# Fixed places for activations and weights, and a longer ordered TensorE table, in a hybrid decoder layer

## The chip, the cores and the metric

The kernel runs on one core of one Trainium2 chip, as one program in one launch. The metric is the device time of one execution in microseconds (us); smaller is better. Engines are called PE (TensorE matmul), PEld (its weight load), DVE (VectorE), ACT (ScalarE), POOL (GpSimd) and SP (the queue that issues most transfers). "L177" is line 177 of the kernel before.

## What is computed

One decoder layer on 256 tokens of width 2048, in float32 (the reference, cut):

```
h = rms_norm(x, attn_norm_g);  proj = h @ w_in                       # 2048 x 4448
r, k, v, w, a, g = split(token_shift(proj[:, :3360], mu))            # RWKV-7 group, 16 heads x 64
y_rwkv = rwkv7_mixer(...)        # a recurrent state per head, group norm, bonus term, gate
c_q, c_kv, k_pe = split(proj[:, 3360:])                              # latent attention, 8 heads x 128
q = rms_norm(c_q) @ w_uq;  kv = rms_norm(c_kv) @ w_ukv               # 512 -> 1536 and 512 -> 2048
y_mla = softmax(causal(q_nope k_nope^T + rope(q_pe) rope(k_pe)^T)) v
x = x + concat(y_rwkv, y_mla) @ w_out                                # 2048 x 2048
h = rms_norm(x, ffn_norm_g)
gate = causal_depthwise_conv3(h @ w_gate);  up = h @ w_up            # 2 x (2048 x 5632)
x = x + (silu(gate) * up) @ w_down                                   # 5632 x 2048
out = rms_norm(x, final_norm_g)
```

## The kernel before

Weights come from HBM in pieces of 128 x 1024 float32 (512 KB). `piece()` loads one into `raw` (SP queue, 3 buffers), ACT casts it to `hi` (L138, the fp32r rounding) and DVE subtracts to get `lo = raw - hi` (L139); `hi` and `lo` have 3 buffers each. Activations are split into the same two halves. A product is then three PE products (hi by hi, hi by lo, lo by hi), each matmul with a 128 x 128 stationary operand that PEld loads and a moving operand of 256 or 512 columns:

- Input projection (`in_tile`, `latent_tile`, L196/L199/L822): the weights are stationary, the activations `x` move, 256 columns at a time.
- Up projections of the latent attention (`up_b`, L896): the weights are stationary, the latents `cl` move, 256 columns.
- Value projection and output projection (`part_a`, L837): the activations (`cl`, `yhi`, `ylo`) are stationary, the weights move, 512 columns.
- First FFN product, gate and up (`prod_b`, L177 for `hi`, 512 columns of `z` hi and lo together; L183 for `lo`, 256 columns). `runs_of` fixes how many `hi` matmuls come ahead of each group of eight `lo` matmuls.
- Down product (`prod_a`, L219 to L221): the activations `hh`, `hl` are stationary, the weights move, 512 columns.

The FFN goes in two blocks, of 24 and 20 tiles of 128 hidden columns; each block is a gate/up stage and then a down stage. PSUM accumulators of the big products are `mm` (3 buffers), small steps use `ch` (3) and `at` (2).

Buffers with the tag `a8` hold 8 x 256 float32 per partition and rotate over four places; in turn they hold the four tiles of `x`, then `qn`, `kn`, `yhi`, `ylo` (second half of the attention output), then the four tiles of `z` (the normed input of the FFN, before its scale), then four weight pieces `wt` that are split early. A counter moves every second one by 32 elements (128 bytes). All other tiles of 1024 elements are `s4`.

Between the input projection and the FFN, PE runs an order that is written out by hand. `STREAM` lists the big products (`l` latent tiles, `q K Q` up projections, `v` values, `W` output projection, first digit the half of the mixed width, second the block of 512 output columns); each is a generator that yields every 8 matmuls of 256 columns or every 4 of 512. `PLAN` says how many such yields to take and which small step comes then: `R` and `T` (`corner_r`, `corner_t`: 32 x 32 matmuls that finish the inverse of the recurrence; `R` reads `T11`, which comes from DRAM through `dU`, L636 to L638), `w x i s u o` (the recurrence by chunks of 64 tokens), `r b` (norms of the latents), `c e` (rotary part), `S P A` (scores, transposes of the probabilities, attention times values), `N G Y` (group norm, gate, transposes of y), `X` (`turn_x`: transposes of the new x into `z`) and `g` (four loads on the ACT queue). The FFN follows that table, where the tile scheduler places it.

The second norm's factor `rs2B` is needed to scale the results of the gate/up product when they leave PSUM (`joined`), not to start it; it is computed after the table on POOL (`rsqrt` without an engine) and spread by two small matmuls (`bcast`, L262).

Of the kernel before, what the change touches and what calls it, by code (L numbers as in the profile page):

```python
# [54 lines left out]
def hybrid_layer(ctx: ExitStack, tc: tile.TileContext, a: dict, out: bass.AP):  # L55
# [73 lines left out]

    def piece(src, dst=None):  # L130
# [7 lines left out]
        S.copy(hi, raw)  # L138
# [24 lines left out]


    def prod_b(n, src, act, done):


        pcs, accs, g = {}, {}, 0
        for q, run in enumerate(runs_of(2 * n)):
            for _ in range(run):  # L170
                p, j = divmod(g, 8)
                i, h = divmod(p, 2)
                if j == 0:
                    pcs[p] = piece(src(i, h))
                    if h == 0:
                        accs[i] = mm()
                PE.matmul(accs[i], pcs[p][0][:, j * P:(j + 1) * P], act(h * 8 + j), start=h == 0 and j == 0,  # L177
                          stop=False, skip_group_check=True)
                g += 1
            i, h = divmod(q, 2)  # L180
            lo = pcs.pop(q)[1]
            for j in range(8):
                PE.matmul(accs[i][:, :T], lo[:, j * P:(j + 1) * P], act(h * 8 + j)[:, 0, :], start=False,  # L183
                          stop=h == 1 and j == 7, skip_group_check=True)
            if h == 1:
                done(i, accs.pop(i))

    def runs_of(n):
        full, tail = (10, 8) + (9, 9, 6) * 7 + (6,), (10, 8, 9, 6, 9, 9, 6, 7)
        return full * (n // 24) + tail * (n % 24 // 8)  # L190

# [698 lines left out]
    def up_b(src, i, x, dsts):  # L890
        pcs = piece(a[src][i])
        accs = [mm() for _ in range(2)]
        ops = [(j, q, k, s) for j in range(2) for q, k, s in
               [(0, k, s) for k in range(4) for s in range(2)] + [(1, k, 0) for k in range(4)]]
        for m, (j, q, k, s) in enumerate(ops):
            PE.matmul(accs[j][:, :T], pcs[q][:, (j * 4 + k) * P:(j * 4 + k + 1) * P], cl[x][k // 2][:, k % 2, s, :],  # L896
                      start=m % 12 == 0, stop=m % 12 == 11)
# [132 lines left out]
    def turn_x(c, j):  # L1030
        if not zs:
            zs.extend(hl4("z", 1) for _ in range(4))
        pt = ch("pxT").rearrange("p (k t) -> p k t", k=2)
# [4 lines left out]
        for k in range(2):  # L1038
# [3 lines left out]
            V.scalar_tensor_tensor(zs[c][:, j * 2 + k, 1, :], pt[:, k, :], vv("fg", kt),  # L1042
                                   hv.bitcast(F32), ALU.mult, ALU.subtract)
# [44 lines left out]
    V.tensor_reduce(ss2, ssf.rearrange("p (b c) -> p b c", b=2), AX.X, ALU.add)
# [24 lines left out]
    for blk, nf in enumerate((24, 20)):
        hh = [s4(F32R, "hh").rearrange("p (k t) -> p k t", k=4) for _ in range(nf // 4)]
        hl = [s4(F32R, "hl").rearrange("p (k t) -> p k t", k=4) for _ in range(nf // 4)]
        gates = {}

        def ffn_tile(i, acc):
            fi = i // 2
            f = f0 + fi  # L1120
            if i % 2 == 0:
                gates[fi] = acc
                return
            gt = hbuf()
            joined(gt[:, 2:258], gates.pop(fi), rs2B)
            cv = t1("cv")
            S.activation(cv, gt[:, 2:258], AF.Identity, bias=vv("cb", f), scale=vv("c2", f))
            V.scalar_tensor_tensor(cv, gt[:, 1:257], vv("c1", f), cv, ALU.mult, ALU.add)
            V.scalar_tensor_tensor(cv, gt[:, 0:256], vv("c0", f), cv, ALU.mult, ALU.add)
            S.activation(cv, cv, AF.Silu)  # L1130
            up = t1("up")
            joined(up, acc, rs2B)
            V.tensor_tensor(up, up, cv, ALU.mult)
            hv = hh[fi // 4][:, fi % 4, :]
            S.copy(hv, up)
            V.tensor_tensor(hl[fi // 4][:, fi % 4, :], up, hv.bitcast(F32), ALU.subtract)

        prod_b(2 * nf, lambda i, h: a["wgu"][f0 + i // 2, i % 2, h], z_hl, ffn_tile)
# [113 lines left out]
```

## Time and profile before

| | |
|---|---|
| time, median of 3 runs | 1185.33 us (1184.88 to 1186.14) |
| the profiled execution | 1185.31 us, of which its span (first to last instruction) 1183.5 us |
| TensorE clock granted, mean | 0.995 |
| PE / PEld / DVE / ACT / POOL busy | 98% / 86% / 68% / 51% / 2% |
| HBM read | 210.58 MB |

Stages in the profiled execution, in us from the span's start: input projection with the RWKV preparation to about 200, recurrence and latents to about 275, attention and output projection to about 445, gate/up of block one to 711, down of block one to 842, gate/up of block two to 1065, down of block two to the end. A PE row of the trace is busy for longer than the step to the next matmul, since matmuls overlap; the step from start to start is what counts on PE, and it is what the readings below use.

### The profile page before, as it was taken

The numbers are of one execution on the slowest core, as the hardware profiler recorded it, in microseconds if no ns is written. First come the engines' busy times: TensorE is split into PE (matmuls) and PEld (weight loads), VectorE is DVE, ScalarE is ACT, GpSimd is POOL, SyncE is SP. The second block draws the span as 40 slices with busy tenths as digits, with TensorE's granted clock in tenths as the row PEclk, the third lists the DMA queues.
The fourth block names the chain that finished last, engine by engine and source line by source line (L and its number), as shares of the span: only waits on it lengthen the run. The fifth ranks groups of instructions, "written<-read, shape, count | busy, mean of one in ns | idle before, by whom it ended". The sixth has DMA issues, their size and how long they took to land.

```text
span 1183.5 us, 19464 instructions
## 1 busy us (share of the span) xinstructions
PE 1164.0 (98%) x7669; PEld 1022.3 (86%) x7669; DVE 803.8 (68%) x1318; ACT 608.6 (51%) x906; POOL 22.0 (2%) x59
## 2 busy tenths in 40 slices
PE   9999999999999999999999999999999999999996
PEld 9899999898977778888888888888888888888885
DVE  6897669646886567777777775444577777775563
ACT  6884346345553456555555554333455555554441
POOL 1200000000000001000000000000000000000000
PEclk9999999899999999999999999999999999999999
DMA  8545456616435545655555555566556555566672
GB/s 330 191 145 176 134 161 190 197 52 192 155 124 178 173 165 179 192 188 190 195 186 189 196 180 194 195 194 193 190 189 195 187 187 195 187 225 210 200 216 84
DMA packets 71132, 215.99 MB, mean 182 GB/s; under 512 B 17616, under 2 KB 18000, under 8 KB 71040
## 3 DMA queue, kind: packets, MB, share of 16 engines
q1 hardware_dynamic: 69920, 211.97, 55.3%
q10 hardware_dynamic: 768, 2.05, 0.6%
q8 instruction: 60, 0.98, 0.3%
q0 software_dynamic: 352, 0.72, 0.2%
q14 instruction: 32, 0.26, 0.1%
HBM read 210.58 MB, written 3.41 MB: 181 GB/s over the span
## 4 chain that ended last, share of the span: by engine, by line
PE 91%; DMA 3%; DVE 3%; ACT 2%; issue 0%; SPq 0%; ACTq 0%; DVEq 0%
PE mm L177 28%; PE mm L183 14%; PE mm L837 8%; PE mm L221 7%; PE mm L220 7%; PE mm L219 7%; PE mm L196 6%; PE mm L822 3%; PE mm L199 3%; PE mm L896 2%; DMA raw<-in_win 1%; PE pg L570 1%; DVE lo L139 1%; ACT hi L138 1%; PE py L714 1%; PE px L714 1%
## 5 line engine op out<-in xcount | busy, mean ns | idle before, releaser
L139 DVE TENSOR_TENSOR lo<-raw,hi 128x1024 fp32r<-128x1024 f32 x376 | 459.7, 1223 | 274.7 <-ACT hi L138 201.5
L138 ACT CAST hi<-raw 128x1024 fp32r<-128x1024 f32 x376 | 395.1, 1052 | 428.4 <-PE mm L177 137.6
L177 PE MATMUL mm<-z,hi 128*128 128x512 f32 x1408 | 355.2, 393 | 1.0 <-DVE z L1042 1.0
L177 PEld LDWEIGHTS mm<-z,hi 128*128 128x128 f32 x1408 | 251.6, 188 | 47.3 <-DVE z L1042 1.2
L183 PEld LDWEIGHTS mm<-z,lo 128*128 128x128 f32 x1408 | 189.2, 188 | 14.8
L183 PE MATMUL mm<-z,lo 128*128 128x256 f32 x1408 | 192.6, 279 | 0.0
L221 PE MATMUL mm<-hi,hl 128*128 128x512 f32 x336 | 130.7, 389 | 0.0
L220 PE MATMUL mm<-lo,hh 128*128 128x512 f32 x336 | 130.7, 389 | 0.0
L219 PE MATMUL mm<-hi,hh 128*128 128x512 f32 x336 | 119.7, 389 | 0.0
L196 PE MATMUL mm<-x,hi 128*128 128x256 f32 x768 | 102.9, 282 | 0.0
L196 PEld LDWEIGHTS mm<-x,hi 128*128 128x128 f32 x768 | 93.7, 188 | 1.6 <-issue 0.3
L221 PEld LDWEIGHTS mm<-hi,hl 128*128 128x128 f32 x336 | 63.1, 188 | 13.1
L220 PEld LDWEIGHTS mm<-lo,hh 128*128 128x128 f32 x336 | 63.1, 188 | 13.1
L219 PEld LDWEIGHTS mm<-hi,hh 128*128 128x128 f32 x336 | 63.1, 188 | 13.0
L199 PE MATMUL mm<-x,lo 128*128 128x256 f32 x384 | 55.2, 281 | 0.0
L837 PE MATMUL mm<-hi,yhi 128*128 128x512 f32 x128 | 50.9, 397 | 0.0
L837 PE MATMUL mm<-lo,yhi 128*128 128x512 f32 x128 | 50.7, 396 | 0.0
L837 PE MATMUL mm<-hi,ylo 128*128 128x512 f32 x128 | 50.5, 395 | 0.2 <-DVE ylo L978 0.2
L199 PEld LDWEIGHTS mm<-x,lo 128*128 128x128 f32 x384 | 48.7, 188 | 1.4 <-issue 1.3
L822 PE MATMUL mm<-x,hi 128*128 128x256 f32 x256 | 34.5, 285 | 0.0
L822 PEld LDWEIGHTS mm<-x,hi 128*128 128x128 f32 x256 | 31.8, 193 | 0.5
L837 PEld LDWEIGHTS mm<-lo,yhi 128*128 128x128 f32 x128 | 24.1, 188 | 6.2 <-issue 1.5
(284 smaller groups left out, 1121.6 us busy)
## 6 DMA issues: line engine op xcount, KB each, us to landing
raw<-in_wgu SPq DMA_DIRECT2D x176, 512.0 KB, 3.4
raw<-in_wdn SPq DMA_DIRECT2D x88, 512.0 KB, 4.2
raw<-in_win SPq DMA_DIRECT2D x70, 512.0 KB, 3.9
raw<-in_wout SPq DMA_DIRECT2D x32, 512.0 KB, 3.4
raw<-in_wuq SPq DMA_DIRECT2D x6, 512.0 KB, 4.2
xraw<-in_xT SPq DMA_DIRECT2D x4, 512.0 KB, 6.8
xt<-in_x SPq DMA_DIRECT2D x4, 512.0 KB, 6.9
raw<-in_wuv SPq DMA_DIRECT2D x4, 512.0 KB, 4.4
```

Source lines behind the costliest of these rows:

```text
L138: S.copy(hi, raw)
L139: last_lo[0] = V.tensor_tensor(lo, raw, hi.bitcast(F32), ALU.subtract).ins
L177: PE.matmul(accs[i], pcs[p][0][:, j * P:(j + 1) * P], act(h * 8 + j), start=h == 0 and j == 0, stop=False, skip_group_check=True)
L183: PE.matmul(accs[i][:, :T], lo[:, j * P:(j + 1) * P], act(h * 8 + j)[:, 0, :], start=False, stop=h == 1 and j == 7, skip_group_check=True)
L196: PE.matmul(acc[:, :T], hi[:, j * P:(j + 1) * P], act(kt0 + j)[:, s, :], start=first and j == 0 and s == 0, stop=False)
L199: i = PE.matmul(acc[:, :T], lo[:, j * P:(j + 1) * P], act(kt0 + j)[:, 0, :], start=False, stop=last and j == n - 1)
L219: PE.matmul(accs[tb], ah, wh, start=first and j == 0, stop=False)
L220: PE.matmul(accs[tb], ah, wl, start=False, stop=False)
L221: i = PE.matmul(accs[tb], al, wh, start=False, stop=last and j == n - 1)
L714: PE.matmul(dst[HS[h], a_ * 64:(a_ + 1) * 64], lhsT, rhs, start=begin and a_ == 0, stop=True, skip_group_check=True)
L822: PE.matmul(acc[:, :T], w[:, j * P:(j + 1) * P], act(j)[:, s, :], start=first and m == 0, stop=last and m == len(ops) - 1)
L837: PE.matmul(accs[tb], act, w, start=first and j == 0 and act is ah and w is wh, stop=last and j == 1 and act is al)
```

## The change

- `a8` tiles no longer rotate: each of the four places has its own tag and each use names its place (`x` 0 to 3, `qn` 0, `kn` 3, `ylo` 1, `yhi` 2, `z` 0 to 3, `wt` 0 to 3). The offset in a tile is named too: 0 for `x`, `qn`, `kn`, 16 elements (64 bytes) for `yhi`, `ylo`, `wt`, 32 elements (128 bytes) for `z`. `hi` and `lo` buffers grow from 1024 to 1088 elements; the pieces of `up_b` start 16 elements in.
- The first FFN block's gate/up stage becomes a generator `ffn_up` and the last entry, `F`, of `STREAM`. Its first four half pieces come as (tile 0, half 0), (tile 1, half 0), (tile 0, half 1), (tile 1, half 1), so the first matmuls need only `z` tiles 0 and 1; the runs of `hi` matmuls at its start change to 9, 9, 6, 10, 8.
- The second norm becomes a small step `n` of the table, and its reciprocal root goes from POOL to DVE.
- `PLAN` and a few neighbours in `STREAM` (q1 before q0, K3 before Q3) are rewritten. `gate_loads` waits for the first chunk's output (`ylast[0]`), not the fourth's.

```diff
-    def a8(n, dt=F32R, off=0):
-        u = sb.tile([P, 8 * T + 32], dt, tag="a8", name=nm(n), bufs=4)
-        o = 32 * ((na8[0] + off) % 2)
-        na8[0] += 1
-        return u[:, o:o + 8 * T].rearrange("p (k t) -> p k t", t=T)
+    def a8(slot, n, dt=F32R, off=0):
+        u = sb.tile([P, 8 * T + 64], dt, tag=f"a8_{slot}", name=nm(n), bufs=1)
+        return u[:, off:off + 8 * T].rearrange("p (k t) -> p k t", t=T)
...
-    xs_ = [hl4("x") for _ in range(4)]
+    xs_ = [hl4(g, "x") for g in range(4)]
...
-            hi = sb.tile([P, 1024], F32R, tag="hi", name=nm("hi"), bufs=NHI)
-            lo = sb.tile([P, 1024], F32R, tag="lo", name=nm("lo"), bufs=NLO)
+            hi = sb.tile([P, 1088], F32R, tag="hi", name=nm("hi"), bufs=NHI)[:, off:off + 1024]
+            lo = sb.tile([P, 1088], F32R, tag="lo", name=nm("lo"), bufs=NLO)[:, off:off + 1024]
...
-                       "qn": lambda: a8("qn", F32), "kn": lambda: a8("kn", F32),
+                       "qn": lambda: a8(0, "qn", F32), "kn": lambda: a8(3, "kn", F32),
...
-                       "yh1": lambda: a8("yhi"), "yl1": lambda: a8("ylo")}[n]()
+                       "yh1": lambda: a8(2, "yhi", off=16), "yl1": lambda: a8(1, "ylo", off=16)}[n]()
...
-        pcs = piece(a[src][i])
+        pcs = piece(a[src][i], off=16)
...
-        with tc.issue_after(ylast[3]):
+        with tc.issue_after(ylast[0]):
...
-            zs.extend(hl4("z", 1) for _ in range(4))
+            zs.extend(hl4(c, "z", 32) for c in range(4))
...
+            elif k == "F":
+                yield from ffn_up(0, NFS[0], RUNS[0], [(0, 0), (1, 0), (0, 1), (1, 1)] + PAIRS[4:])
...
-    25 w00 3 r0 4 R0 R1 2 T0 w01 1 i00 i01 u00 w11 u01 w10 o01 T1 x10 x11 o00 s10 i10 i11 s11 u10 u11
+    12 w00 18 r0 4 R0 R1 T0 w01 1 i00 i01 w11 u00 u01 w10 o01 T1 x11 x10 o00 s10 i10 i11 s11 u10 w20 u11
...
-    bcast(rsqrt(ss2, 1.0 / DM, EPS, 2), rs2B)
+    def norm2():
+        ss2 = st("ss2f", 2)
+        V.tensor_reduce(ss2, ssf.rearrange("p (b c) -> p b c", b=2), AX.X, ALU.add)
+        bcast(rsqrt(ss2, 1.0 / DM, EPS, 2, V), rs2B)
...
+    NFS = (24, 20)
+    SYNC = (10, 8) + (9, 9, 6) * 7 + (6,)
+    RUNS = ((9, 9, 6, 10, 8) + (9, 9, 6) * 6 + (6,) + SYNC * 3, SYNC * 3 + (10, 8, 9, 6, 9, 9, 6, 7))
...
-                    held.append((q, piece(a["wdn"][3, f0 // 2 + q], a8("wt", off=1))))
+                    held.append((q, piece(a["wdn"][3, f0 // 2 + q], a8(c, "wt", off=16))))
```

The places below are those that the prediction speaks of. Names are `out<-moving,stationary`, with the buffers' numbers. PE at the first `R` (the matmul that needs `T11`), before and then after:

```order
L822 MATMUL mm_2876<-x_67,lo_2920 128x256 x4
L822 MATMUL mm_2876<-x_68,lo_2920 128x256 x4
L822 MATMUL mm_2972<-x_65,hi_2975 128x256 x8
L822 MATMUL mm_2972<-x_66,hi_2975 128x256 x8
L676 MATMUL pR_2995<-T_2158,G_1384 32x32
```

```order
L790 MATMUL mm_2973<-x_65,hi_2976 128x256 x8
L790 MATMUL mm_2973<-x_66,hi_2976 128x256 x8
L790 MATMUL mm_2973<-x_65,lo_2977 128x256 x4
L790 MATMUL mm_2973<-x_66,lo_2977 128x256 x4
L790 MATMUL mm_2973<-x_67,hi_3006 128x256 x8
L644 MATMUL pR_3018<-T_2158,G_1384 32x32
```

Sixteen matmuls of 256 columns, which stood behind the `R` and `T` steps, now stand ahead of `R`; no big matmul is left between `R` and `T`.

PE at the last two heads of the attention (`ptp` transposes of the probabilities, `po` attention times values), before and then after:

```order
L837 MATMUL mm_4383<-hi_4464,yhi_4115 128x512
L837 MATMUL mm_4383<-lo_4465,yhi_4115 128x512
L837 MATMUL mm_4383<-hi_4464,ylo_4117 128x512
L968 MATMUL ptp_4492<-cst,pexp_4443 128x128 x3
L975 MATMUL po_4497<-pT_4491,vm_3844 128x256
L976 MATMUL po_4497<-pT_4491,vm_3846 128x128
```

```order
L936 MATMUL ptp_4478<-cst,pexp_4378 128x128 x3
L805 MATMUL mm_4365<-hi_4465,ylo_4228 128x512
L805 MATMUL mm_4366<-hi_4465,yhi_4226 128x512
L805 MATMUL mm_4366<-lo_4466,yhi_4226 128x512
L805 MATMUL mm_4366<-hi_4465,ylo_4228 128x512
L936 MATMUL ptp_4488<-cst,pexp_4444 128x128 x3
L943 MATMUL po_4493<-pT_4477,vm_3854 128x256
L944 MATMUL po_4493<-pT_4477,vm_3856 128x128
L943 MATMUL po_4498<-pT_4487,vm_3854 128x256
```

The last `po` no longer follows its own transposes at once: the `po` of the head before stands between, and that one has four 512-column matmuls of cover.

PE at the end of the output projection and the start of the FFN (`pxT` transposes of x), before and then after:

```order
L1037 MATMUL pxT_5141<-cst,x_4460 128x128 x4
L1037 MATMUL pxT_5150<-cst,x_4460 128x128 x4
L177 MATMUL mm_5284<-z_5118,hi_5280 128x512
L1037 MATMUL pxT_5159<-cst,x_4697 128x128 x4
L837 MATMUL mm_5081<-lo_5134,yhi_4674 128x512
```

```order
L805 MATMUL mm_5095<-hi_5179,ylo_4708 128x512
L1005 MATMUL pxT_5210<-cst,x_4687 128x128 x4
L1058 MATMUL mm_5225<-z_5021,hi_5221 128x512 x4
L1058 MATMUL mm_5225<-z_5022,hi_5221 128x512 x4
L1005 MATMUL pxT_5234<-cst,x_4783 128x128 x4
```

The single FFN matmul that stood in the middle of the output projection is gone from there; the first FFN matmuls now come behind the last output-projection matmul, and the last transposes behind eight of them.

More of the change, by code (lines that the diff above doesn't have):

```diff
@@ L76, in sv, with hl4 @@
         return sb.tile([P, 1024], F32, tag="sv", name=nm(n), bufs=3)
-    na8 = [0]
-    def a8(n, dt=F32R, off=0):
-        u = sb.tile([P, 8 * T + 32], dt, tag="a8", name=nm(n), bufs=4)
-        o = 32 * ((na8[0] + off) % 2)
-        na8[0] += 1
-        return u[:, o:o + 8 * T].rearrange("p (k t) -> p k t", t=T)
-    def hl4(n, off=0):
-        return a8(n, off=off).rearrange("p (k s) t -> p k s t", s=2)
+    def a8(slot, n, dt=F32R, off=0):
+        u = sb.tile([P, 8 * T + 64], dt, tag=f"a8_{slot}", name=nm(n), bufs=1)
+        return u[:, off:off + 8 * T].rearrange("p (k t) -> p k t", t=T)
+    def hl4(slot, n, off=0):
+        return a8(slot, n, off=off).rearrange("p (k s) t -> p k s t", s=2)
     def t1(n, w=T, dt=F32):
@@ L127, in hybrid_layer, with piece @@
     nc.scalar.dma_start(vec, a["vec"])
-    def piece(src, dst=None):
+    def piece(src, dst=None, off=0):
         raw = sb.tile([P, 1024], F32, tag="raw", name=nm("raw"), bufs=NRAW)
@@ L161, in flush @@
             f()
[L165 to L190, printed above, removed]
     def prod_c(acc, pieces, act, kt0, n, first, last):
@@ L1043, in turn_x, with ffn_up, ffn_tile @@
                                    hv.bitcast(F32), ALU.mult, ALU.subtract)
+    rs2B = sb.tile([P, T], F32, tag="rsB", name="rs2B", bufs=1)
+    def norm2():
+        ss2 = st("ss2f", 2)
+        V.tensor_reduce(ss2, ssf.rearrange("p (b c) -> p b c", b=2), AX.X, ALU.add)
+        bcast(rsqrt(ss2, 1.0 / DM, EPS, 2, V), rs2B)
+    z_hl = lambda k: zs[k // 4][:, k % 4, :, :]
+    def ffn_up(f0, nf, runs, order):
+        gates, pcs, accs, seen, g = {}, {}, {}, set(), 0
+        def ffn_tile(i, acc):
+            fi = i // 2
+            f = f0 + fi
+            if i % 2 == 0:
+                gates[fi] = acc
+                return
+            gt = hbuf()
+            joined(gt[:, 2:258], gates.pop(fi), rs2B)
+            cv = t1("cv")
+            S.activation(cv, gt[:, 2:258], AF.Identity, bias=vv("cb", f), scale=vv("c2", f))
+            V.scalar_tensor_tensor(cv, gt[:, 1:257], vv("c1", f), cv, ALU.mult, ALU.add)
+            V.scalar_tensor_tensor(cv, gt[:, 0:256], vv("c0", f), cv, ALU.mult, ALU.add)
+            S.activation(cv, cv, AF.Silu)
+            up = t1("up")
+            joined(up, acc, rs2B)
+            V.tensor_tensor(up, up, cv, ALU.mult)
+            if fi % 4 == 0:
+                hs_.append([s4(F32R, n).rearrange("p (k t) -> p k t", k=4) for n in ("hh", "hl")])
+            hv = hs_[-1][0][:, fi % 4, :]
+            S.copy(hv, up)
+            V.tensor_tensor(hs_[-1][1][:, fi % 4, :], up, hv.bitcast(F32), ALU.subtract)
+        hs_ = []
+        held_h.append(hs_)
+        for q, run in enumerate(runs):
+            for r in range(run):
+                p, j = divmod(g, 8)
+                i, h = order[p]
+                if j == 0:
+                    pcs[p] = piece(a["wgu"][f0 + i // 2, i % 2, h])
+                    if i not in accs:
+                        accs[i] = mm()
+                PE.matmul(accs[i], pcs[p][0][:, j * P:(j + 1) * P], z_hl(h * 8 + j), start=i not in seen,
+                          stop=False, skip_group_check=True)
+                seen.add(i)
+                g += 1
+                if r % 4 == 3 and r < run - 1:
+                    yield
+            yield
+            i, h = order[q]
+            last = (i, 1 - h) in order[:q]
+            lo = pcs.pop(q)[1]
+            for j in range(8):
+                PE.matmul(accs[i][:, :T], lo[:, j * P:(j + 1) * P], z_hl(h * 8 + j)[:, 0, :], start=False,
+                          stop=last and j == 7, skip_group_check=True)
+            if last:
+                ffn_tile(i, accs.pop(i))
+            yield
@@ L1045, in stream @@
+    held_h = []
+    NFS = (24, 20)
+    SYNC = (10, 8) + (9, 9, 6) * 7 + (6,)
+    RUNS = ((9, 9, 6, 10, 8) + (9, 9, 6) * 6 + (6,) + SYNC * 3, SYNC * 3 + (10, 8, 9, 6, 9, 9, 6, 7))
+    PAIRS = [(i, h) for i in range(48) for h in range(2)]
     def stream():
@@ L1085, in hybrid_layer @@
             pass
-    ss2 = st("ss2f", 2)
-    V.tensor_reduce(ss2, ssf.rearrange("p (b c) -> p b c", b=2), AX.X, ALU.add)
-    rs2B = sb.tile([P, T], F32, tag="rsB", name="rs2B", bufs=1)
-    bcast(rsqrt(ss2, 1.0 / DM, EPS, 2), rs2B)
-    z_hl = lambda k: zs[k // 4][:, k % 4, :, :]
     fgb = [None, None]
@@ L1112, in hybrid_layer @@
     f0 = 0
[L1113 to L1138, printed above, removed]
+    for blk, nf in enumerate(NFS):
+        if blk == 1:
+            for _ in ffn_up(f0, nf, RUNS[1], PAIRS[:2 * nf * 2]):
+                pass
+        hs = held_h[blk]
         if blk == 1:
@@ L1143, in hybrid_layer @@
                     nc.sync.dma_start(fgb[i], a["fng"][:, i * 1024:(i + 1) * 1024].broadcast_to([P, 1024]))
-        h_hi = lambda k: hh[k // 4][:, k % 4, :]
-        h_lo = lambda k: hl[k // 4][:, k % 4, :]
+        h_hi = lambda k: hs[k // 4][0][:, k % 4, :]
+        h_lo = lambda k: hs[k // 4][1][:, k % 4, :]
         n = nf // 2
```

13 lines of the change are left out of this document (7 added, 6 removed).

## The prediction

> **What bounds the kernel now.** I read the page's busy shares and chain first, then the waits of PE, then the step from matmul to matmul, since the first two leave nothing else to gain.
>
> ```profile
> PE 1164.0 (98%) x7669; PEld 1022.3 (86%) x7669; DVE 803.8 (68%) x1318; ACT 608.6 (51%) x906; POOL 22.0 (2%) x59
> PE 91%; DMA 3%; DVE 3%; ACT 2%; issue 0%; SPq 0%; ACTq 0%; DVEq 0%
> ```
>
> PE is busy for 98% of the span and is 91% of the chain that ended last; DVE at 68% and ACT at 51% only matter where PE waits for them. The change removes no matmul, so it can act in three ways: PE's few waits, PE's clock, and the step between two matmuls.
>
> PE's waits (in all, times, longest, us):
>
> ```profile
> PE pR L676 <- DMA T<-dU: 2.4, 2, 1.8
> PE po L975 <- ACT pT L969: 1.8, 2, 1.2
> PE mm L896 <- ACT qn L886: 1.4, 2, 0.9
> PE mm L177 <- DVE z L1042: 1.0, 1, 1.0
> ```
>
> Those four are 6.6 us, the rest under 2.5. Steps: two stretches of the span (length, then busy time of PE and its matmul count), the first one gate/up, the second down.
>
> ```profile
> 512.04:578.75 66.71, 66.71 (x386) 58.38 (x385) 48.03 (x72) 37.13 (x55) 0.00 (x0) 1.00 0.57 190
> 720.00:840.00 120.00, 120.00 (x531) 99.41 (x530) 57.49 (x51) 46.41 (x44) 0.00 (x0) 1.00 0.60 193
> ```
>
> The first is one full cycle of 24 pieces, 192 matmuls of 512 columns and 192 of 256 (the count has two more that lie over its ends): 347.4 ns for a pair. In the second, all are of 512 columns; the count includes one that was already running for up to 0.39 us, so (120 + 0.39) / 531 = 226.7 ns each. Four consecutive runs of the gate/up stage:
>
> ```profile
> 504.69 1.78 PE L177 MATMUL mm<-z,hi 128*128 128x512 f32 x7
> 506.32 1.10 PE L183 MATMUL mm<-z,lo 128*128 128x256 f32 x8
> 507.26 1.54 PE L177 MATMUL mm<-z,hi 128*128 128x512 f32 x6
> 508.64 1.07 PE L183 MATMUL mm<-z,lo 128*128 128x256 f32 x8
> 509.55 1.55 PE L177 MATMUL mm<-z,hi 128*128 128x512 f32 x6
> ```
>
> From start to start: seven of 512 columns in 1.63 us (232.9 ns), eight of 256 in 0.94 (117.5), six of 512 in 1.38 (230.0), eight of 256 in 0.91 (113.8). The same form of matmul takes 226.7 in one stage and 230 to 233 in the other, and there are two speeds for 256 columns. What differs is where the operands lie. In the built program all of down's operands (`hi`, `lo`, `hh`, `hl`) start at 224 modulo 256 bytes; `z` tiles start at 32 or 160. So a pair could take 226.7 + 113.8 = 340.5; the FFN's 44 tiles of 32 pairs, 1408, are 9.7 us above that.
>
> **Part 1: sixteen matmuls ahead of R, none between R and T.**
>
> ```profile
> 223.90 2.05 PE L822 MATMUL mm<-x,hi 128*128 128x256 f32 x16
> 227.75 0.22 PE L676 MATMUL pR<-T,G 32*32 32x32 f32 x2 [1.80 <-DMA T<-dU]
> 228.54 3.50 PE L676 MATMUL pR<-T,G 32*32 32x32 f32 x126 [0.57 <-DMA T<-dU]
> 231.97 2.08 PE L822 MATMUL mm<-x,lo 128*128 128x256 f32 x8
> 233.84 1.89 PE L822 MATMUL mm<-x,hi 128*128 128x256 f32 x8
> 235.66 1.20 PE L689 MATMUL pT<-TT,RT 32*32 32x32 f32 x64
> 236.78 0.69 PE L714 MATMUL px<-UV,G 128*64 128x64 f32 x16
> 228.80:235.60 6.80, 6.80 (x138) 6.59 (x132) 2.59 (x3) 1.15 (x2) 0.00 (x0) 0.50 0.65 184
> ```
>
> PE waits 1.80 us for the first half of `T11` and 0.57 for the second. Sixteen matmuls at 2.05 / 16 = 0.12 us are 1.9 us, more than the first wait: **-1.8**; the second stays, since that half lands later. SP's order ahead of `T11` is unchanged, and the operands of the sixteen are cast by then (their piece's transfer stands ahead of `dU` in both orders).
>
> The last row is a stretch with its granted clock: 0.50 for 6.8 us, right behind the wait. Two costs hang on it. The sixteen matmuls from 231.97 to 235.66 take 3.69 us where the same sixteen took 1.9: 1.8. The 126 records of R take 3.43 where T, the same tile size at full clock, does 64 in 1.12, so 126 in 2.2: 1.2. Without the wait I take the clock as kept: **-3.0**. The ends are 0 and -3.0.
>
> The wait was 2.4 us and halved the clock for 6.8. [...]
>
> Cover is lost behind R: T reads what ACT and DVE copy out of R's PSUM. T follows R's second half at once, and its own half was copied during it; the accumulator of the step after T waits for the other copy: **+0.3** (ends 0 and +1.1, the length of T).
>
> **Part 2: up projections, attention.**
>
> ```profile
> 292.52 1.22 PE L896 MATMUL mm<-cl,hi 128*128 128x256 f32 x8 [0.46 <-ACT qn L886]
> 295.15 1.22 PE L896 MATMUL mm<-cl,hi 128*128 128x256 f32 x8 [0.93 <-ACT qn L886]
> 293.99 1.22 DVE L777 TENSOR_TENSOR bv<-bv,gnb 128x1024 f32<-128x1024 f32 x1
> 295.13 0.74 DVE L209 TENSOR_TENSOR kn<-mm,rrB 128x256 f32<-128x256 f32 x2
> ```
>
> PE waits 0.46 and 0.93 for an accumulator. What holds it is DVE: the copy-out of `kn` (L209) starts only behind 1.22 us pieces of rotary and bonus work. In the changed order of DVE the factor's copy stands ahead of two such pieces and `kn` ahead of two others: half is saved, **-0.7** (0 to -1.4).
>
> ```profile
> 347.20 0.49 PE L968 MATMUL ptp<-cst,pexp 128*128 128x128 f32 x3
> 348.87 0.70 PE L975 MATMUL po<-pT,vm 128*128 128x256 f32 x2 [1.19 <-ACT pT L969]
> 347.40 1.04 ACT L138 CAST hi<-raw 128x1024 fp32r<-128x1024 f32 x1 [0.43 <-PE mm L837]
> 348.35 0.47 ACT L969 COPY pT<-ptp 128x384 f32<-128x384 f32 x1
> ```
>
> The last `po` waits 1.19 us, since ACT has a 1.04 us cast ahead of the 0.47 us copy it needs; the one before it waited 0.62 (the waits above: 1.8 in all). Now four matmuls of 0.23 us and the next transposes cover one, and one `po` of some 0.6 us the other: **-1.0** (0 to -1.8). In return `N` of the first half moves seven yields ahead, and its 1.2 us pieces on DVE now lie among the softmax steps; the price is in "new waits".
>
> **Part 3: the seam to the FFN.**
>
> ```profile
> 435.14 1.03 PE L1037 MATMUL pxT<-cst,x 128*128 128x128 f32 x8
> 437.15 0.49 PE L177 MATMUL mm<-z,hi 128*128 128x512 f32 x1 [0.98 <-DVE z L1042]
> 437.98 0.63 PE L1037 MATMUL pxT<-cst,x 128*128 128x128 f32 x4 [0.34 <-issue]
> ```
>
> A single FFN matmul sits in the output projection and waits 0.98 us for `z`; the transposes behind it lose 0.34 more. It leaves that place: **-1.3**. At the end the last transposes now have eight matmuls (1.85 us) of cover for the last two adds to x, on DVE, 512 columns each: by the row of L209 (0.74 us for two of 256) about 1.5 us and their latency, so **+0.3** (0 to +1.3).
>
> The norm moves from POOL to DVE.
>
> ```profile
> 447.23 0.19 POOL L238 TENSOR_SCALAR rm<-ss2f 128x2 f32<-128x2 f32 x1 [162.21 <-DVE ss2f L1088]
> 451.92 0.20 POOL L253 TENSOR_TENSOR ry<-ry,rt 128x2 f32<-128x2 f32 x1
> 222.23 0.15 DVE L870 TENSOR_TENSOR ssm<-pss,rs 128x2 f32<-128x2 f32 x1
> 226.20 0.16 DVE L872 SCALAR_TENSOR_TENSOR rr<-ry,rs 128x2 f32<-128x2 f32 x1
> ```
>
> POOL's 14 steps take 4.9 us. On DVE a like chain takes 4.1 with other work in between. Its result is needed only when the first gate tile leaves PSUM; with three accumulators the fourth is asked for some 6 us later. Cost **0** (ends -0.2 and +1.2, one DVE step like L777's, if one `lo` comes too late for PE behind the chain). The gate loads are only released earlier: 0, hidden by a stage that waits for its own products.
>
> **Part 4: places.**
>
> ```profile
> 350.00:364.00 14.00, 14.00 (x63) 11.48 (x62) 1.00 0.45 152
> 402.00:432.00 30.00, 30.00 (x134) 24.83 (x133) 1.00 0.57 191
> 276.43 0.64 PE L896 MATMUL mm<-cl,lo 128*128 128x256 f32 x4
> 276.91 1.12 PE L896 MATMUL mm<-cl,hi 128*128 128x256 f32 x8
> ```
>
> The output projection (first row: half with `y` in `a8`, second: half with `y` in `s4`) steps at 14.39 / 63 = 228.4 and 30.39 / 134 = 226.8. `yhi` and `ylo` now start at 224 modulo 256, like the weights: 192 matmuls x 1.6 ns = **-0.3**. In the up projections weights and `cl` both start at 224, and the step is 0.48 / 4 = 120.0 ns: slower than any 256-column run whose operands differ. Their weights move to 32: 240 x (120.0 - 115.6, the middle of 113.8 and 117.5) = **-1.1** (-1.5 to -0.6). So equal places help 512 columns and hurt 256.
>
> `z` feeds both. Half its tiles stay at 32 relative to weights at 224, half move there from 160. For a pair the ends are 340.5 (-9.7 us) and 232.9 + 120.0 = 352.9 (+7.7). The nearest row is today's 347.4, half of which is already this place; I take **-0.5**.
>
> [...]
>
> **Sum.** -1.8 - 3.0 + 0.3 - 0.7 - 1.0 - 1.3 + 0.3 + 0 - 0.3 - 1.1 - 0.5 = -9.1. Against it I set **+1.5** for new waits that the old trace cannot show: some forty small steps have new neighbours, and the four old waits had a mean of 1.65; one of these is 1.5 (ends 0 and +4). That is -7.6 on the execution's 1185.31, which stands 0.02 under the median: **1177.7 us**.
>
> **Rivals.**
> 1. The clock halves all the same: PE has R, R and T on end. +3.0: 1180.7. For it: the clock stayed halved through R. Against: the wait it began with is mostly gone.
> 2. The `z` places lock the gate/up stage at its fast step, which a third of the runs show already: 9.2 us more, 1168.5. Against: only half of the tiles move, to a place that half have today.
> 3. The order's waits return elsewhere (PE behind DVE, where norm and softmax now mix): parts 1 to 3 give nothing, part 4 gives 1.9: 1183.4, or up to 1186 with the new waits. Against: the longest wait is on a transfer, not on an engine.
> [...]
> 5. Slower: the new spacing of weight buffers (4352 bytes, not 4096) costs. Down's operands are then no longer equal modulo 512, and `z` may lock slow. Price: 1056 matmuls x (120.0 - 113.8) = 6.5, and 7.7 + 0.5 for the pairs: 1192.4. It decides (over 1187.7) from 10.0 us, 2.6 ns on each of these 3872 matmuls. For it: the places' effect is large and known at few distances. Against: `x` tiles at 160 and 416 modulo 512 go by without a change of step.
>
> **Chances.** The forecast 0.46 (own range 1174 to 1181), rival 1 0.15, 2 0.10, 3 0.15, 4 0.05, 5 0.09. A measurement here tells about 0.2%, 2.4 us. Faster by more: the forecast, 1, 2, 4 and a little of 3, 0.78; within: the rest of 3, 0.13; slower: 5, 0.09. Leaving out half of 2, a part of 3 and 5 gives 1169 to 1184.
>
> **What would show it.** Part 1: the wait of `pR` falls from 2.4 us to about 0.6, and no stretch near 230 us is granted 0.50. Part 2: the waits for `qn` and `pT` fall to half together. Part 3: no `z` matmul before the last `W`, and the first gate/up `hi` without a wait. Part 4: up projections step at 114 to 118 ns, both halves of the output projection at 226.7, the 24-piece cycle at 66.6 us with down still at 226.7. A cycle far from 66.7 us, or down above 227, makes the prediction wrong by itself; so does a new PE wait of over 3 us.

## The result, and the profile after

The changed kernel takes 1173.40 us (median of 6 runs, 1172.28 to 1174.38) against 1185.11 (6 runs, 1182.26 to 1186.23): the ratio is 0.9903, with a 95% interval of 0.9890 to 0.9917. It is 11.7 us faster; 7.6 were forecast. The span of the profiled execution went from 1183.5 to 1171.5 us. The busy line and the chain line of the page (engines' busy time; share of the chain that ended last):

```profile
PE 1155.2 (99%) x7669; PEld 1017.3 (87%) x7669; DVE 805.8 (69%) x1329; ACT 607.2 (52%) x906; POOL 18.2 (2%) x45
PE 91%; DVE 3%; DMA 2%; ACT 2%; issue 1%; SPq 0%; ACTq 0%; DVEq 0%
```

PE is busy for 8.8 us less with the same 7669 instructions, and it still makes up 91% of the chain. So most of the gain can't be waits that were removed; matmuls follow one another faster. One row of a stretch shows it, the same 220 us inside the first gate/up stage, before and then after (length, then busy time of PE and its matmul count):

```profile
470.00:690.00 220.00, 220.00 (x1269) 192.56 (x1267) 158.69 (x239) 122.76 (x178) 0.00 (x0) 1.00 0.58 190
```

```profile
470.00:690.00 220.00, 220.00 (x1285) 193.58 (x1284) 160.54 (x241) 124.64 (x182) 0.00 (x0) 1.00 0.59 192
720.00:830.00 110.00, 110.00 (x487) 91.06 (x486) 53.15 (x47) 42.80 (x41) 0.00 (x0) 1.00 0.63 194
```

1269 matmuls before, 1285 after. Half of them have 512 columns and half 256, and the count takes in one that had already been running for up to 0.39 us (0.3 is taken here): a pair takes 2 x 220.3 / 1269 = 347.2 ns before and 342.9 after. For 1408 pairs that is 6.1 us. The second row after is the down stage: (110 + 0.39) / 487 = 226.7 ns, as before.

PE's waits after (in all, times, longest, us):

```profile
PE po L943 <- ACT pT L937: 1.0, 2, 0.5
PE ptp L936 <- DVE pexp L928: 0.9, 1, 0.9
PE mm L1058 <- DVE z L1010: 0.8, 1, 0.8
PE mm L864 <- ACT qn L854: 0.5, 1, 0.5
PE pT L657 <- ACT RT L648: 0.4, 1, 0.4
PE pT L657 <- DMA TT<-dT: 0.3, 1, 0.3
```

The wait of `pR` for `T11` (2.4) is gone, that for `qn` fell from 1.4 to 0.5, that for `pT` from 1.8 to 1.0. New are 0.9 for `pexp` and 0.7 ahead of the `T` step. PE at the place of `R` and `T` (start, length, instructions, idle time before), and the clock in the 16 us around it:

```profile
225.90 1.10 PE L790 MATMUL mm<-x,hi 128*128 128x256 f32 x8
226.93 2.52 PE L644 MATMUL pR<-T,G 32*32 32x32 f32 x128
229.83 0.24 PE L657 MATMUL pT<-TT,RT 32*32 32x32 f32 x2 [0.37 <-ACT RT L648]
230.39 1.80 PE L657 MATMUL pT<-TT,RT 32*32 32x32 f32 x62 [0.31 <-DMA TT<-dT]
232.12 1.12 PE L682 MATMUL px<-UV,G 128*64 128x64 f32 x16
226.00:242.00 16.00, 15.18 (x431) 13.94 (x431) 6.83 (x15) 5.67 (x13) 0.00 (x0) 0.79 0.46 127
```

`R` follows the big matmuls without a wait. Yet the mean granted clock of the 16 us is 0.79: (1 - 0.79) x 16 x 2 = 6.7 us at half speed, as many as before. `T` takes 1.80 us for 62 where 64 took 1.20 before.

The up projections: eight matmuls in 0.91 us, four in 0.45, about 113 ns each, where 120.0 stood. The output projection of the first half: 18 steps in 4.08 us, 226.7 ns, where the mean was 228.4.

```profile
285.21 1.07 PE L864 MATMUL mm<-cl,hi 128*128 128x256 f32 x8
286.12 0.62 PE L864 MATMUL mm<-cl,lo 128*128 128x256 f32 x4
286.57 1.07 PE L864 MATMUL mm<-cl,hi 128*128 128x256 f32 x8
...
349.76 0.39 PE L805 MATMUL mm<-hi,yhi 128*128 128x512 f32 x1
353.84 0.39 PE L805 MATMUL mm<-hi,yhi 128*128 128x512 f32 x1
```

The seam to the FFN:

```profile
436.77 0.60 PE L1005 MATMUL pxT<-cst,x 128*128 128x128 f32 x4
437.12 2.10 PE L1058 MATMUL mm<-z,hi 128*128 128x512 f32 x8
443.86 0.50 PE L1058 MATMUL mm<-z,hi 128*128 128x512 f32 x1 [0.79 <-DVE z L1010]
```

The last transposes of the output projection and the first FFN matmuls follow one another without a wait, as forecast; the wait for `z` now comes 7 us after the first of them, at the last tiles, and is 0.79 us instead of 0.98 + 0.34.

### The profile page after: what moved, and what is told of

Read it like the earlier page. It is cut to its first block, busy times and chain, and to the rows that moved or that the text cites. A ratio compares the mean times of both kernels' runs of the same rounds, so it can differ in the third digit from the quotient of the medians.

```text
span 1171.5 us, 19456 instructions
## 1 busy us (share of the span) xinstructions
PE 1155.2 (99%) x7669; PEld 1017.3 (87%) x7669; DVE 805.8 (69%) x1329; ACT 607.2 (52%) x906; POOL 18.2 (2%) x45
## 3 DMA queue, kind: packets, MB, share of 16 engines
HBM read 210.58 MB, written 3.41 MB: 183 GB/s over the span
## 4 chain that ended last, share of the span: by engine, by line
PE 91%; DVE 3%; DMA 2%; ACT 2%; issue 1%; SPq 0%; ACTq 0%; DVEq 0%
PE mm L1058 27%; PE mm L1069 14%; PE mm L805 8%; PE mm L189 7%; PE mm L187 7%; PE mm L188 7%; PE mm L164 6%; PE mm L790 3%; PE mm L167 3%; PE mm L864 2%; PE pg L538 1%; PE px L682 1%; DMA raw<-in_win 1%; PE py L682 1%; DVE lo L134 1%
## 5 line engine op out<-in xcount | busy, mean ns | idle before, releaser
L1069 PEld LDWEIGHTS mm<-z,lo 128*128 128x128 f32 x1408 | 186.4, 188 | 14.9
L1069 PE MATMUL mm<-z,lo 128*128 128x256 f32 x1408 | 189.1, 276 | 0.0
L805 PEld LDWEIGHTS mm<-hi,ylo 128*128 128x128 f32 x128 | 24.0, 188 | 6.7 <-issue 1.5
```

The source lines that it names most:

```text
L805: PE.matmul(accs[tb], act, w, start=first and j == 0 and act is ah and w is wh, stop=last and j == 1 and act is al)
L1069: PE.matmul(accs[i][:, :T], lo[:, j * P:(j + 1) * P], z_hl(h * 8 + j)[:, 0, :], start=False, stop=last and j == 7, skip_group_check=True)
```

## The experiments

Two questions were open. Where do 6 us in gate/up come from, when the place of half the `z` tiles had been valued at 0.5? And why did the clock still halve? In the table, "excess" is what a matmul takes over 226.67 ns (512 columns) or 113.33 ns (256), the mean over the gate/up stages of the profiled execution, from the steps from start to start between two matmuls of the same run. "Distance" is how far the weights start behind `z`, modulo 256 bytes, in the built program. The weights of the gate/up product start at 224 in all these kernels, so this column names places of `z` as well as distances; the runs on `z` cannot tell the two apart.

| kernel | distance of z | excess 512 / 256, ns | time, us (runs) | ratio to before, 95% |
|---|---|---|---|---|
| before | 64 and 192 | 4.4 / 3.1 | 1183.61 to 1185.11 | 1 |
| after | 192 | 2.1 / 0.6 | 1173.40 (6) | 0.9903 (0.9890 to 0.9917) |
| old places | 64 and 192 | 4.4 / 3.0 | 1179.68 (10) | 0.9973 (0.9961 to 0.9985) |
| old spacing | 192 | 2.1 / 0.6 | 1172.47 (4) | 0.9919 (0.9902 to 0.9937) |
| z mixed | 64 and 192 | 4.4 / 3.0 | 1179.79 (10) | 0.9974 (0.9963 to 0.9985) |
| z at 64 | 64 | 6.1 / 2.1 | 1180.15 (10) | 0.9977 (0.9966 to 0.9987) |
| z equal | 0 | 3.9 / 5.6 | 1181.82 (10) | 0.9983 (0.9973 to 0.9993) |
| z at 128 | 128 | 5.8 / 5.5 | 1184.41 (10) | 1.0006 (0.9997 to 1.0016) |
| z at 160, cover between | 160 | 6.2 / 6.3 | 1186.38 (10) | 1.0022 (1.0011 to 1.0033) |
| before, new places | 192 | 2.0 / 0.6 | 1177.41 (4) | 0.9944 (0.9922 to 0.9965) |
| cover between R and T | 192 | 2.1 / 0.6 | 1171.64 (4) | 0.9896 (0.9878 to 0.9913) |
| cover ahead of R | 192 | 2.1 / 0.6 | 1176.78 (5) | 0.9938 (0.9925 to 0.9951) |
| all 256-column products at 192 | 192 | 2.1 / 0.6 | 1174.88 (6) | 0.9919 (0.9903 to 0.9934) |
| norm on POOL | 192 | 2.1 / 0.7 | 1172.57 (5) | 0.9899 (0.9883 to 0.9914) |

### Places against order: the two crossed kernels

The changed kernel with the old places:

```diff
-            hi = sb.tile([P, 1088], F32R, ...)[:, off:off + 1024]
+            hi = sb.tile([P, 1024], F32R, ...)          # lo likewise; up_b's offset goes with it
-"yh1": lambda: a8(2, "yhi", off=16), "yl1": lambda: a8(1, "ylo", off=16)
+"yh1": lambda: a8(2, "yhi"), "yl1": lambda: a8(1, "ylo")
-zs.extend(hl4(c, "z", 32) for c in range(4))
+zs.extend(hl4(c, "z", (0, 0, 32, 32)[c]) for c in range(4))
-a8(c, "wt", off=16)
+a8(c, "wt", off=32 * (c % 2))
```

> The changed kernel with every place put back modulo 256 bytes: the first two tiles of z at 160 and the others at 32, y half 1 and wt at 160 and 32, weights of the up projections at 224 like cl, hi and lo buffers 4096 bytes apart. The order is the changed one. Theory 'places pay as measured after': the gate/up stages take 263 and 222.3 us for the counts they have now less the 2 us of matmuls that come before the first lo, so about 5.2 us of gate/up, 1.0 of up_b and 0.3 of the output projection come back: 1173.4 + 6.5 = 1179.9. Rival 'the order alone': what PE's neighbours do sets the step, not the place: 1173.4, with the gate/up cycle unchanged.

And the kernel before with the new places alone:

```diff
-    def a8(n, dt=F32R, off=0):                    # rotating, every second one 32 elements in
+    def a8(slot, n, dt=F32R, off=0):              # as in the change, with all its uses
...
-pcs = piece(a[src][i])
+pcs = piece(a[src][i], off=16)
```

> The kernel before, with only the places of the change (a8 tiles in four fixed places with named offsets, hi and lo of 1088 elements, up_b 16 elements in); order and table as before. Theory 'places and order add up': the places were worth 6.3 us between the kernel with old places and the changed one: 1183.7 (the median of before in the last 46 runs) - 6.3 = 1177.4. Rival 'the places only pay in the new order (the FFN in the table)': 1183.7.

Measured: 1179.68 and 1177.41, as the theory of places had it (1179.9 and 1177.4). The stretch of 220 us in each:

```profile
470.00:690.00 220.00, 220.00 (x1268) 192.58 (x1267) 158.15 (x238) 122.74 (x178) 0.00 (x0) 1.00 0.55 190
```

```profile
470.00:690.00 220.00, 220.00 (x1285) 193.52 (x1284) 160.84 (x241) 124.44 (x181) 0.00 (x0) 1.00 0.56 194
```

The count is 1268 and 1285: it goes with the places, not with the order. So the places are worth 6.3 us in the new order (1179.68 - 1173.40) and about 7 in the old one (1184.87, the runs of before beside it, to 1177.41), and the order about 4 (1183.77, the runs of before beside the first, to 1179.68). The rival that the neighbours in the order set the step is out.

### Which of the places

```diff
-            hi = sb.tile([P, 1088], F32R, ...)[:, off:off + 1024]
+            hi = sb.tile([P, 1024], F32R, ...)          # lo likewise; up_b's offset goes with it
```

> The changed kernel with hi and lo buffers 4096 bytes apart again (all at 224 modulo 512) and up_b's weights at 224 like cl; z, y and wt stay at their new places. Theory 'distance of z modulo 256': only up_b comes back, 240 x 4.2 ns = 1.0: 1174.4, gate/up step as in the changed kernel (230.0 a pair's two columns aside: excess 2.0 ns for 512 columns and 0.6 for 256). Rival 'the 4352-byte spacing spreads the weights': gate/up falls back too, 5.2 + 1.0: 1179.6.

```diff
-zs.extend(hl4(c, "z", 32) for c in range(4))
+zs.extend(hl4(c, "z", (0, 0, 32, 32)[c]) for c in range(4))
```

> The changed kernel with z tiles 0 and 1 at 160 modulo 256 (offset 0) and 2 and 3 at 32 (offset 32 elements), as the kernel before had them; spacing of hi and lo as changed. Theory 'distance of z': the gate/up stages fall back to their old excess, 5.2 us: 1178.6. Rival 'spacing': 1173.4.

```diff
-zs.extend(hl4(c, "z", 32) for c in range(4))
+zs.extend(hl4(c, "z", 0) for c in range(4))
```

> The changed kernel with all four z tiles at 160 modulo 256 (offset 0), that is 64 bytes behind the weights' 224 instead of 192. Theory 'it is the distance': the kernel before had 5.3 ns (512 columns) and 2.7 ns (256) of excess per matmul at 64, now 2.0 and 0.6 at 192: 1408 x (3.2 + 2.05) = 7.4 us: 1180.8. Rival 'any place will do if all tiles have the same': 1173.4 with the same steps.

```profile
470.00:690.00 220.00, 220.00 (x1285) 193.57 (x1284) 160.58 (x242) 124.62 (x182) 0.00 (x0) 1.00 0.57 192
```

```profile
470.00:690.00 220.00, 220.00 (x1269) 192.58 (x1269) 158.81 (x239) 123.21 (x179) 0.00 (x0) 1.00 0.55 189
```

```profile
470.00:690.00 220.00, 220.00 (x1265) 191.53 (x1264) 158.06 (x237) 122.24 (x178) 0.00 (x0) 1.00 0.55 190
```

1285 with the old spacing of the weight buffers, 1269 with mixed `z`, 1265 with all of `z` at 64: the 4352-byte spacing has no part in it, and "all tiles alike" isn't enough. The place of `z` alone carries 6.4 us (1179.79 - 1173.40), and all of `z` at 64 took 1180.15 where 1180.8 had been expected. The old spacing also puts `up_b`'s weights back on `cl`'s place; in its trace their excess is 6.1 ns again, 1.0 us, but the median does not show it (1172.47, four runs, against 1173.40): that much lies within what the clock does between executions (below).

Then the other places. The prediction had said that equal places help 512 columns and hurt 256:

```diff
-zs.extend(hl4(c, "z", 32) for c in range(4))
+zs.extend(hl4(c, "z", 16) for c in range(4))      # distance 0; with 48: 128
```

> The changed kernel with all z tiles at 224 modulo 256 (offset 16 elements), where the weights start: distance 0. Theory 'equal places help 512 columns and hurt 256' (as down and the old up projections show): 512 columns fall from 2.0 ns of excess to 0, 256 columns rise from 0.6 to 6.2: 1408 x (-2.0 + 5.6) = +5.1 us: 1178.5. Rival 'equal is best for both when the tiles are all alike': 1173.4 - 3.8 = 1169.6.

> The changed kernel with all z tiles at 96 modulo 256 (offset 48 elements): distance 128, for which no row exists yet. The steps known at 0, 64 and 192 give bounds: no excess at all is 1173.4 - 1408 x 2.7 ns = 1169.6; as bad as the worst of both seen (5.7 and 6.2) is 1173.4 + 1408 x 9.2 ns = 1186.4. Theory 'distance decides, nearest neighbour is 192 or 64': between the two, 1173.4 to 1180.2. Rival 'only the half of 128 bytes matters': 128 is as 0, 1178.5.

```diff
-zs.extend(hl4(c, "z", 32) for c in range(4))
+zs.extend(hl4(c, "z", 40) for c in range(4))      # distance 160
-4 R0 R1 T0 w01 ... 6 r1
+4 R0 R1 1 T0 w01 ... 5 r1                         # as in "cover between", below
```

> The changed kernel with the yield between R and T (1171.6 as measured), and all z tiles at offset 40 elements: 64 modulo 256, distance 160, half way between the good 192 and the bad 128. Theory 'the step changes smoothly with distance': about half of the 11 us between them: 1177. Rival 'it goes by steps of 64 bytes, rounded down to 128': 1171.6 + 11 = 1182.6. Rival 'rounded up to 192': 1171.6.

```profile
470.00:690.00 220.00, 220.00 (x1260) 193.53 (x1259) 158.18 (x237) 122.09 (x178) 0.00 (x0) 1.00 0.55 189
```

```profile
470.00:690.00 220.00, 220.00 (x1252) 192.07 (x1251) 156.95 (x235) 121.59 (x177) 0.00 (x0) 1.00 0.54 188
```

```profile
470.00:690.00 220.00, 220.00 (x1249) 191.66 (x1248) 156.43 (x236) 120.78 (x176) 0.00 (x0) 1.00 0.57 187
```

1260 at distance 0, 1252 at 128, 1249 at 160; 1285 at 192. All three expectations on the mechanism missed. Equal places hurt 256 columns as said (5.6 ns), but 512 columns had 3.9 ns there, not 0. And it is no smooth function: 32 bytes away from the best place lies the worst one. What stays is an empirical list of five places, of which the change took the best. (The kernel with `z` at 160 was run on another chip than the other variants; the kernel before took 1184.58 us beside it.)

Does the list hold for another product?

```diff
-4 R0 R1 T0 w01 ... 6 r1
+4 R0 R1 1 T0 w01 ... 5 r1
-xs_ = [hl4(g, "x") for g in range(4)]
+xs_ = [hl4(g, "x", 32) for g in range(4)]
-pcs = piece(a[src][i], off=16)
+pcs = piece(a[src][i], off=48)
```

> The changed kernel with the yield between R and T, x tiles moved from 160 to 32 modulo 256 (offset 32 elements) and up_b's weights from 32 to 160 (offset 48 elements), so that every 256-column product has its weights 192 bytes ahead of its moving operand, as z. Theory 'distance 192 is good for 256 columns whatever the operand': x's excess falls from about 2.0 ns at 64 to the 0.6 of z at 192: 1680 x 1.4 = 2.3 us, cl's from 2.1 to 0.6: 240 x 1.5 = 0.4: 1171.6 - 2.7 = 1168.9. Rival 'only gate/up, where all columns are read in a fixed cycle, profits': 1171.6.

It does not: 1174.88, where the same kernel with `x` and `cl` at 64 takes 1171.64. By the steps of the trace `x` went from 1.7 ns of excess to 4.1, `cl` from 2.0 to 4.5: 1680 x 2.4 + 240 x 2.5 = 4.6 us lost, of which 3.2 are seen in the time. Here `x` starts at 32 and its weights at 224, which are the very places of `z` and its weights in the changed kernel, where 256 columns have 0.6 ns. So neither the distance nor the two places by themselves set the step. Rows of one form of matmul show that one distance has no one price. First `x` at 64, in the kernel with the yield between `R` and `T`:

```profile
21.99 1.98 PE L164 MATMUL at<-x,hi 128*128 128x256 f32 x16
23.80 1.07 PE L167 MATMUL at<-x,lo 128*128 128x256 f32 x8
25.15 2.15 PE L164 MATMUL mm<-x,hi 128*128 128x256 f32 x16 [0.28 <-ACT hi L133]
27.14 1.10 PE L167 MATMUL mm<-x,lo 128*128 128x256 f32 x8
28.08 2.05 PE L164 MATMUL mm<-x,hi 128*128 128x256 f32 x16
29.97 1.10 PE L167 MATMUL mm<-x,lo 128*128 128x256 f32 x8
```

Then `x` at 192:

```profile
28.63 2.05 PE L164 MATMUL mm<-x,hi 128*128 128x256 f32 x16
30.51 1.10 PE L167 MATMUL mm<-x,lo 128*128 128x256 f32 x8
```

At 64, sixteen matmuls take 23.80 - 21.99 = 1.81 us, 113.1 ns each. Then PE waits 0.28 us, and behind the wait sixteen of the same form take 29.97 - 28.08 = 1.89 us, 118.1 ns each, with the operands at the same places modulo 256. At 192 they take 1.88, 117.5 each. In these rows there are two speeds, and each lasts for many matmuls; here the change of speed coincides with a short wait. That the wait made it is not shown, and what picks a speed is open. A place may do no more than make one of them likelier; no run tests that.

### The clock at R and T

```diff
-4 R0 R1 T0 w01 ... 6 r1
+4 R0 R1 1 T0 w01 ... 5 r1
```

> The changed kernel with one yield (8 matmuls of 256 columns) put between R and T, taken from the six ahead of r1. Theory 'small matmuls of 32 x 32 and short waits are idle for the clock': the stretch from the last big matmul to the first 64 x 64 step, 226.9 to 232, is broken in two, each under 3.4 us, so the clock is kept in every execution (mean 0.998) and the 0.7 us of waits of pT are covered too: about 1.5 to 3 us less in the executions that had the dip, 1173.4 to about 1171. Rival 'the clock falls by the wait alone': the same gain also in the kernel with the yield ahead of R. Rival 'the clock falls whatever stands there': 1173.0.

```diff
-4 R0 R1 T0 w01 ... 6 r1
+5 R0 R1 T0 w01 ... 5 r1
```

> The changed kernel with the same yield put ahead of R instead, so R and T still follow one another but start 0.9 us later, when T's transfer has landed. Theory 'small matmuls count as idle': 128 + 64 matmuls of 32 x 32 on end still take 3.6 us and the clock still falls in most executions: 1173.4 less 0.3 of waits, 1173.1. Rival 'waits decide': no dip, about 1171.

PE with the yield between, and its clock:

```profile
226.77 2.37 PE L644 MATMUL pR<-T,G 32*32 32x32 f32 x128
229.07 1.19 PE L790 MATMUL mm<-x,hi 128*128 128x256 f32 x8
230.19 1.20 PE L657 MATMUL pT<-TT,RT 32*32 32x32 f32 x64
226.00:242.00 16.00, 15.19 (x493) 14.03 (x492) 9.14 (x19) 7.89 (x18) 0.00 (x0) 1.00 0.55 160
```

PE with the yield ahead, its clock, and ACT at the same place:

```profile
228.88 2.21 PE L644 MATMUL pR<-T,G 32*32 32x32 f32 x128
234.42 1.92 PE L657 MATMUL pT<-TT,RT 32*32 32x32 f32 x64 [3.33 <-ACT RT L648]
226.00:242.00 16.00, 12.42 (x306) 11.52 (x306) 6.75 (x17) 4.75 (x8) 0.00 (x0) 0.79 0.50 134
...
232.72 1.04 ACT L133 CAST hi<-raw 128x1024 fp32r<-128x1024 f32 x1 [5.47 <-DMA raw<-in_win]
233.79 1.06 ACT L648 COPY RT<-pR 32x512 f32<-32x512 f32 x2
```

Between `R` and `T` the eight matmuls keep the clock at 1.00, cover the waits ahead of `T`, and give the fastest version here, 1171.64, against the 1171 expected. Its two stretches of small matmuls last 2.30 and 1.75 us. That 3.4 us is the bound below which such a stretch keeps the clock was the author's estimate and is not shown: in the kernel with `z` at 64 the stretch from `R` to the next 256-column matmul, 227.73 to 232.45, waits included, lasts 4.72 us, and the clock stays at 1.00. A new wait of 0.76 us, for the copy of `TT` behind an ACT cast, comes further on. All four executions of this version had a mean clock of 0.998, those of the changed kernel 0.995 or 0.996. Two other kernels of the table have the same yield. With all 256-column products at 192 the six executions have 0.997 or 0.998; with `z` at 160 three of ten have 0.994 to 0.996, and no trace shows where those three lost it. Ahead of `R` the same eight cost 3.4 us, and both times expected (1173.1, 1171) missed. There ACT's cast of a weight piece, which waits 5.47 us for a transfer, stands ahead of the copy of `RT` that `T` needs, so PE waits 3.33 us, and the clock goes down for 6.7 us, as in the changed kernel. So this kernel does not tell whether small matmuls alone, without a wait, halve the clock; the case was spoilt by a new wait.

The lengths tell more. The same 16 us in two kernels whose order at this place is that of the changed one, old places and `z` at 64:

```profile
226.00:242.00 16.00, 15.20 (x468) 13.77 (x468) 7.22 (x16) 6.82 (x15) 0.00 (x0) 0.89 0.44 126
```

```profile
226.00:242.00 16.00, 14.18 (x458) 12.99 (x458) 7.87 (x20) 7.31 (x14) 0.00 (x0) 1.00 0.48 129
```

0.89 is 3.5 us at half speed, 1.00 none, 0.79 (after) 6.7. The halved time comes in portions: 0, 3.4 or 6.8 us, for the same instructions. In 69 executions of the kernel before that ran beside the experiments, the mean clock and the time go together: 0.998, 1180.8 us (median of 2); 0.997, 1181.5 (8); 0.996, 1183.4 (25); 0.995, 1184.8 (25); 0.993, 1186.2 (9). That is the spread of its times, and a part of the scatter of all the times above.

The traces' records of the granted clock show a grid. In the changed kernel the clock changes at 5.30, 230.58, 237.40 and 1165.83 us: 66, 68 and 340 times 3.413 us behind the first change; in the kernel before, the changes stand at 6.88, 228.74, 235.57 and 1177.65 us: 65, 67 and 343 times. In all 14 traces the changes of one execution lie whole multiples of 3.413 us apart, and the first lies anywhere from 4.6 to 6.9 us. So which instructions share one such window of 3.413 us differs from execution to execution.

The windows also tell small matmuls from waits. Each pair of rows is one window and what came behind it, first in the kernel with the old spacing, then with `z` at 64:

```profile
226.47:229.89 3.42, 3.13 (x136) 2.89 (x134) 2.62 (x7) 0.68 (x2) 0.00 (x0) 1.00 1.07 165
229.89:236.72 6.83, 6.74 (x120) 6.30 (x120) 1.79 (x4) 2.75 (x6) 0.00 (x0) 0.50 0.56 211
```

```profile
233.33:236.74 3.41, 2.09 (x51) 1.75 (x52) 0.73 (x2) 1.77 (x3) 0.00 (x0) 1.00 0.18 71
236.74:240.16 3.42, 3.37 (x136) 3.16 (x130) 1.44 (x4) 1.84 (x5) 0.00 (x0) 1.00 0.02 5
```

In the first window PE is idle for only 0.3 us; by the steps, 2.31 us go to `R` and 0.82 to 256-column matmuls, and the clock is halved behind it. In the second PE is idle for 1.32 us, and the clock is kept; it has no 32 x 32 matmul, but 0.26 us of 256 columns and 1.83 us of 64 x 64 and 128 x 64. So the 1.32 us of idle time did not halve the clock by itself, and in these two windows 32 x 32 matmuls counted for less than those. In the ten traces with a halving here, the window ahead of it has at most 0.82 us of 128 x 128 matmuls. Every window at full clock with 1.5 us or more of `R` or `T` that was not followed by a halving has at least 0.88 us of them; the yield between `R` and `T` gives each such window at least 1.13. This is read from traces of one kernel and its variants, not tested by a run of its own.

### The norm on POOL

```diff
-bcast(rsqrt(ss2, 1.0 / DM, EPS, 2, V), rs2B)
+bcast(rsqrt(ss2, 1.0 / DM, EPS, 2), rs2B)
```

> The changed kernel with the second norm's reciprocal root on POOL again. Theory of the prediction 'moving it is worth nothing': 1173.4, PE's wait for z stays 0.8 us. Rival 'the chain on DVE holds up the last z': in the trace after, six steps of the chain (1.2 us) stand ahead of the last lo and z on DVE, and PE waits 0.79 us for z: without them the wait goes and the time is 1172.6. Rival 'POOL is too slow now': the 4.9 us chain ends after the first gate tile needs it, up to 1 us slower.

```profile
PE mm L1058 <- DVE z L1010: 0.7, 1, 0.7
```

1172.57, 0.8 below the changed kernel, which would be the rival's number. But the wait that the rival takes away is still 0.7 us. Two of the five executions had a clock of 0.998 (1172.1 both); the other three, at 0.996, have a mean of 1172.9, and the three of the changed kernel at 0.996 one of 1172.7. So moving the norm is worth nothing that can be seen, as forecast, and the difference of the medians is the clock's.

## Why the prediction was right or wrong

The direction held, and the time lies in the wide range given (1169 to 1184), a little under the forecast's own (1174 to 1181). That it came so near is in part luck: two terms failed in opposite directions.

- **The places of `z` (-0.5; the bounds were -9.7 and +7.7).** This is the term that was mis-sized: it is worth -6.4. The step that failed is "the nearest row is today's 347.4, half of which is already this place". The tiles at 192 had an excess of 3.3 and 3.4 ns while the others stood at 64; with all at 192 they have 2.1 and 0.6. A mean over a mixture did not give the price of its pure half. The prediction's own sign for this term failed too: the 24-piece cycle takes 192 x 342.9 ns = 65.8 us, not 66.6, and it had called a cycle far from 66.7 proof against itself. Rival 2, with 0.10, came close: two thirds of its 9.2 us came.
- **The clock (-3.0).** It failed in the profiled execution: 6.8 us at half speed before and after, as rival 1 had it. The step was "without the wait I take the clock as kept". The other end given for this term, 0, was nearer. The window ahead of the halving had 2.4 us of waits and 0.4 of `R` before; after, it has 0.8 us of waits and 2.7 of `R` and `T`, and none of 128 x 128. Nor does one execution price this term: the same instructions spend 0, 3.4 or 6.8 us at half speed, while the first change of the clock lies anywhere from 4.6 to 6.9 us.
- **The wait for `T11` (-1.8, with 0.57 left).** 2.4 went. The second half no longer lands late: its transfers were issued until 225.3 us before and until 222.7 after, below. In return `T` waits 0.7 us, where 0.3 had been set.

```profile
L638 SPq DMA_DIRECT2D T<-dU x2: 511/1232/1954, 223.2 to 225.3; - x2
```

```profile
L606 SPq DMA_DIRECT2D T<-dU x2: 563/634/705, 222.0 to 222.7; - x2
```

- **Up projections and attention (-0.7, -1.0).** -0.9 and -0.8, by the rows of waits.
- **The seam (-1.3 + 0.3).** The old place is free of the waits, but the last tiles of `z` are late by 0.79 now: -0.5 in all.
- **`up_b` and the output projection (-1.1, -0.3).** From the traces 240 x 4.1 ns = -1.0, and the step of 226.7 in the first half. The reason given, "equal places help 512 columns and hurt 256", fails as a rule: with `z` equal, 512 columns have 3.9 ns of excess. It described down and the output projection, in which the activations are stationary.
- **New waits (+1.5).** 0.9 for `pexp` and 0.7 ahead of `T`, the latter counted above: the size was right, and all of it small.
- **Rival 5, the slower one (0.09).** The spacing costs nothing: down still takes 226.7 ns, and with the old spacing gate/up is the same. Rival 4, that places don't matter, is out: 1285 against 1249 matmuls in the same 220 us. The runs show that the step depends on places; by what mechanism, no run shows.
- **A reading without consequence.** PE's old waits beside the four named add up to 3.2 us in the list, not to under 2.5; no term rests on it.

Together the waits and places above give -2.4 + 0.7 - 0.9 - 0.8 + 0.9 - 0.5 - 1.0 - 0.3 - 6.4 = -10.7 of the -12.0 between the two spans; the last 1.3 us were not assigned. Order and places apart: -5.7 was forecast for the order (parts 1 to 3 and the new waits), -4.1 measured; -1.9 for the places, -6.3 measured.
